# A two-layer decoder on one Trainium2 core: the second MLP product moved behind the whole first one, as one seven-product scheme summed in PSUM

## The chip, the core and the metric

The kernel runs on one core of one Trainium2 chip. The metric is the device time of one launch, in microseconds (us); less is better. Engines are named as in the profile: PE multiplies matrices (PEld are its weight loads), DVE, ACT and POOL work on elements, SP and POOL issue most transfers. SBUF is the memory on chip, PSUM the small one that PE sums into, in banks of 512 float32 columns by 128 partitions.

## What is computed

A decoder of two layers on 512 tokens of 1024 features, all in float32. Layer 0 mixes tokens by windowed means, layer 1 by a gated unit (SGU). Each layer's modulation comes from a vector c; each ends in an MLP with 4096 hidden features:

```python
def sq_relu_mlp(h, w1, w2):
    return jnp.square(jax.nn.relu(h @ w1)) @ w2

for i in range(DEPTH):
    mod = c_act @ ada_w[i] + ada_b[i]
    sh1, sc1, g1, sh2, sc2, g2 = jnp.split(mod, 6, axis=-1)
    h = modulate(rmsnorm(x, norm_mix_g[i]), sh1, sc1)
    y = pool_mixer(...) if kind == 0 else sgu_mixer(...)
    x = x + g1[:, None, :] * y
    h = modulate(rmsnorm(x, norm_mlp_g[i]), sh2, sc2)
    x = x + g2[:, None, :] * sq_relu_mlp(h, mlp_w1[i], mlp_w2[i])
return rmsnorm(x, final_g)
```

## The kernel before

*Precision.* Each float32 operand is held as a rounded high part and the rest (ACT copies the high part, `wh`, `hb`, `oh`; DVE subtracts it to get the low part, `wl`, `ol`), and `mm3` multiplies high by high, high by low and low by high. So one product is three matmuls, and each weight block of 128x1024 costs one ACT copy and one DVE subtraction (`split`); operands are treated alike by `parts`.

*The MLP*, function `mlp`, works in four chunks c of 1024 hidden features, of two quads j of 512 each. A unit is a piece of work whose matmuls stand together in PE's order:

- An **f unit** computes 128 hidden features of the first product plainly, 24 matmuls of 512 columns, for the first `FROM[i]` quads (3 in layer 0, 2 in layer 1).
- An **s unit** (c, j, m) is one of the seven products by which the other quads are multiplied (Strassen's scheme in Winograd's form; `ORDER` = 1, 5, 6, 3, 7, 2, 4), 24 matmuls of 256 columns. The running weight block is made by adding blocks: for m = 5 and 6 on DVE, for m = 4, and the block of m = 7, by accumulating transfers that POOL issues.
- A **p unit** (c, m) is one of seven products of the second product for chunk c = 0, 1, 2 (`ORDER2`), 24 matmuls of 512 columns: 4 pairs of blocks by two halves of the tokens by three parts. Its weights come from w2 as blocks of 1 MB: plain loads, and accumulating ones on POOL's queue that turn the same tile (`bt`) into the next sum (`CHAIN`). Each unit ends by adding both PSUM banks to y in SBUF (the first visit on ACT, the others on DVE).
- A **q unit** (dh, t) is a plain piece of the second product for chunk 3, 24 matmuls of 512 columns; eight of them, with the weights w2e.

Before, the p units of chunk c stand among the s and f units of chunk c+1, mostly one p unit and then one to three of those, and the q units end the layer. `gated` and `last1` add the result times the modulation's gate to x; `last1` also applies the final norm, and cuts the very last q unit into two parts of 256 columns.

*Other work under the MLP.* The columns of the adaLN product for the following stages (`ada`: a 512 KB load and one DVE instruction of 1024 columns each) are put in at the unit that `COLUMNS` gives.

*What sets the order.* PE's order is the program's. In layer 0, every operation of the MLP is recorded by `Plan` (so it bears line L130 in the profile; the others bear L102), and a list scheduler writes down a fixed order for all engines from a cost table: PE's order is given, each other engine takes the ready operation with the earliest due time. In layer 1 only PE's order is fixed, and the framework schedules the rest. Weight buffers `wh`, `wl` rotate over five.

Of the kernel before, what the change touches and what calls it, by code (L numbers as in the profile page):

```python
# [14 lines left out]
P = 128  # L15
D = 1024
# [13 lines left out]
SHIFT = {"o": 64, "q": 0, "g": 0}  # L30

# [40 lines left out]
COLUMNS = (0, 5, 8, 11, 13, 16, 19, 22, 25, 28, 30, 33, 36, 39, 42, 45, 47, 50, 53, 61, 61, 61, 61, 61)  # L72
LEAD = dict(SP=0.0, POOL=0.0, ACT=9.0, DVE=9.0, PE=13.0, fresh=7.0)
A_PARTS = (0, 0, 1, 2, 7)


class Plan:
# [125 lines left out]
    def run(self, lead):  # L203
# [63 lines left out]

        events, now, free, queue = [], 0.0, {e: lead[e] for e in ready}, 0.0
# [8 lines left out]
        while count < N:  # L277
            moved = True
            while moved:
                moved = False  # L280
                for e in ready:
# [4 lines left out]
                    else:  # L286
                        pick, back = None, []
                        while ready[e]:
                            k, i = heapq.heappop(ready[e])
                            if when[i] <= now + 1e-9 and fits(i):  # L290
                                pick = i
                                break
                            back.append((k, i))
# [24 lines left out]
                    heapq.heappush(events, (end, i))  # L318
                    moved = True
# [29 lines left out]
def decoder_kernel(ctx: ExitStack, tc: tile.TileContext, xtok, vecs, fgrow, ada0, ada1, pool_w, w1s, w1, w1f, w1b, w2, w2e, w_v, w_u, w_o, wsT, lnp, bs, out):  # L349
# [58 lines left out]
    def hparts(gap):  # L408
        t = big.tile([P, 2 * KD * S + GAP], F32R, name="hb", tag="hb")
        return t[:, GAP - gap : GAP - gap + 2 * KD * S].rearrange("p (h k s) -> p h k s", h=2, k=KD)  # L410

    h_ = [hparts(GAP)]

    shift(big, LINE - GAP)
# [9 lines left out]
    def H(k, c):  # L424

        return h_[0][:, 0, k, c], h_[0][:, 1, k, c]
# [558 lines left out]
    def mlp(i, first, extra, last, ending):  # L985
# [3 lines left out]
        with (  # L989
            tc.tile_pool(name="gq", bufs=3) as gq_,  # L990
            tc.tile_pool(name="su", bufs=1) as su_,
            tc.tile_pool(name="pad0", bufs=1) as pad0_,
            tc.tile_pool(name="op", bufs=2) as op_,
            tc.tile_pool(name="pad1", bufs=1) as pad1_,
            tc.tile_pool(name="w2p", bufs=3) as w2p_,
            tc.tile_pool(name="hx", bufs=1) as hx_,
            tc.manual_schedule(engines={PE} if i else ORDERED),
        ):
            gq, su, pad0, op, pad1, w2p, hx = (plan.pool(p, True) for p in (gq_, su_, pad0_, op_, pad1_, w2p_, hx_))
            plan.on = i == 0  # L1000
            shift(pad0, SHIFT["o"])
            shift(pad1, SHIFT["q"] - SHIFT["o"])
# [10 lines left out]
            def new_g(c, j):  # L1013
                g[c, j] = gq.tile([P, 4, S], F32, name="g", tag="g")

            def put(f, po):

                c, q = divmod(f, 8)
                j, p = divmod(q, 4)
                if p == 0:  # L1020
                    new_g(c, j)
                t = g[c, j][:, p]
                A.activation(in_row(t) if len(po.shape) == 2 else t.rearrange("p (r h s) -> p r h s", r=2, h=2), in_turn(po), AF.Relu)
                square(t)

            def quad(c, r, j):

                return g[c, j].rearrange("p a (h r t) -> p a h r t", h=2, r=2)[:, :, :, r]
# [19 lines left out]

            def a_parts(step):


                def a(r, j):
                    return xf[:, 4 * j : 4 * j + 4, 256 * r : 256 * r + 256]
# [16 lines left out]
                if m == 5:  # L1070
                    shift(hx, LINE - GAP)
                o = H(slice(0, 4), slice(256, 512)) if m == 7 else operand(*{5: (hx, "hx"), 6: (big, "x0"), 3: (big, "x1")}[m])
                parts(o, sums_a["t"].pop(m))
                sums_a[m] = o

            def a_sums(step):


                def a(r, j):
                    return h32[0][:, 4 * j : 4 * j + 4, 256 * r : 256 * r + 256]  # L1080

                def operand(pool, tag):
                    t = pool.tile([P, 2, 4, 256], F32R, name="as", tag=tag)
                    return t[:, 0], t[:, 1]

                def minus(o, p, q):
                    V.tensor_tensor(o, p, q, ALU.subtract)

                first, half = slice(0, 256), slice(256, 512)
                if step == 0:  # L1090
                    sums_a.update({1: H(slice(0, 4), first), 2: H(slice(4, 8), first), 4: H(slice(4, 8), half)})
                    shift(hx, LINE - GAP)
                    minus(a(1, 1), a(1, 0), a(1, 1))
                    m, o = 5, operand(hx, "hx")
                elif step == 1:
                    minus(a(1, 1), a(1, 1), a(0, 0))
                    m, o = 6, operand(big, "x0")
                elif step == 2:
                    minus(a(0, 0), a(0, 0), a(1, 0))
                    V.tensor_tensor(a(1, 1), a(1, 1), a(0, 1), ALU.add)  # L1100
                    m, o = 3, operand(big, "x1")
                else:
                    m, o = 7, H(slice(0, 4), half)
                parts(o, a(0, 0) if m == 7 else a(1, 1))
                sums_a[m] = o
# [7 lines left out]
            def blk(c, j, r, n):  # L1113
                if (c, j, r, n) not in blks:
                    blks[c, j, r, n] = raw4(w1b[quad_at(c, j), r, n])
                return blks[c, j, r, n]

            def s_prep(u):
# [20 lines left out]
                more = {1: [(c, j, 0, 1)], 5: [(c, j, 1, 1)], 3: [(c, j, 1, 0)], 7: [(*nxt, 0, 0)], 2: [(*nxt, 0, 1)], 4: [(*nxt, 1, 1)]}.get(m, [])  # L1139
# [7 lines left out]
            def s_run(u, w):  # L1147
# [13 lines left out]
                def block(r, n):  # L1161
                    return g[c, j][:, 2 * n : 2 * n + 2, 256 * r : 256 * r + 256]
# [17 lines left out]
            held = {}  # L1180

            def b_of(c, r, n, chain=False):
                kw = dict(name="bt", tag="bt", bufs=1) if chain else dict(name="b", tag="b", bufs=2)
                t = w2p.tile([P, 4, S], F32, **kw)
                Y.dma_start(t, w2[i, c, r, n])
                return t

            def b_add(t, c, r, n):
                G.dma_start(t, w2[i, c, r, n], accum_op=ALU.add)

            def p_prep(u):
                c, m = u
                B = held

                def s_tile(name):
                    return su.tile([P, 4, 2, P], F32, name=name, tag=name)

                if m == 1:
                    wb = B["t"] = b_of(c, 0, 0, True)
                    a = quad(c, 0, 0)  # L1200
                elif m == 5:
                    wb = B["t"]
                    a = B["s"] = s_tile("s")
                    V.tensor_tensor(a, quad(c, 1, 0), quad(c, 1, 1), ALU.subtract)
                elif m == 6:
                    wb = B["t"]
                    a = B["s"]
                    V.tensor_tensor(a, a, quad(c, 0, 0), ALU.subtract)
                    B["b12"] = b_of(c, 0, 1)
                    b_add(B["b12"], c, 1, 1)  # L1210
                    B["u"] = s_tile("u")
                    V.tensor_tensor(B["u"], quad(c, 0, 0), quad(c, 1, 0), ALU.subtract)
                elif m == 3:
                    wb = b_of(c, 1, 1)
                    a = B.pop("s")
                    V.tensor_tensor(a, quad(c, 0, 1), a, ALU.add)
                elif m == 7:
                    wb = B.pop("b12")
# [504 lines left out]
```

## Time and profile before

| | |
|---|---|
| Median of 3 runs | 817.22 us (816.99 to 818.46) |
| Span of the profiled execution | 814.3 us |
| Busy in the span | PE 798.3, PEld 723.5, DVE 686.5, ACT 486.7, POOL 69.1 us |
| Granted PE clock | 0.998 |
| Transfers | 185.47 MB, 228 GB/s |

The profiled execution has no time of its own beside its span; the runs' median lies 2.9 us above it, which covers what comes before the first and after the last recorded instruction. A span is counted from the first recorded instruction; "busy" is the sum of an engine's instructions, and instructions of DVE that follow each other overlap a little in the records, so that the price of one is the distance of two starts where the engine never waits. The page's chain goes back from the last instruction, at each step to what released it.

### The profile page before, as it was taken

The numbers are of one execution on the slowest core, as the hardware profiler recorded it, in microseconds if no ns is written. First come the engines' busy times: TensorE is split into PE (matmuls) and PEld (weight loads), VectorE is DVE, ScalarE is ACT, GpSimd is POOL, SyncE is SP. The second block draws the span as 40 slices with busy tenths as digits, with TensorE's granted clock in tenths as the row PEclk, the third lists the DMA queues.
The fourth block names the chain that finished last, engine by engine and source line by source line (L and its number), as shares of the span: only waits on it lengthen the run. The fifth ranks groups of instructions, "written<-read, shape, count | busy, mean of one in ns | idle before, by whom it ended". The sixth has DMA issues, their size and how long they took to land.

```text
span 814.3 us, 12668 instructions
## 1 busy us (share of the span) xinstructions
PE 798.3 (98%) x4909; PEld 723.5 (89%) x4909; DVE 686.5 (84%) x931; ACT 486.7 (60%) x708; POOL 69.1 (8%) x96
## 2 busy tenths in 40 slices
PE   6999999999999999999999999999999999999996
PEld 5678889999999999888889889999999999999985
DVE  5989888989999999866898886788789988987865
ACT  5476786766666676366233237776867666677521
POOL 4000011010100110000010001010101100111001
PEclk9999999999999999999999999999999999999999
DMA  9989988899898796537755646857888889887402
GB/s 352 417 297 327 403 226 174 274 223 278 233 271 247 185 279 225 195 111 252 242 184 208 219 155 241 302 109 207 206 260 218 230 226 252 212 176 249 139 1 104
DMA packets 43788, 185.47 MB, mean 228 GB/s; under 512 B 4920, under 2 KB 5072, under 8 KB 36432
## 3 DMA queue, kind: packets, MB, share of 16 engines
q1 hardware_dynamic: 35280, 137.72, 46.6%
q0 software_dynamic: 8016, 44.58, 27.4%
q10 hardware_dynamic: 432, 2.36, 0.7%
q8 instruction: 39, 0.64, 0.3%
q14 instruction: 21, 0.17, 0.1%
HBM read 178.33 MB, written 6.30 MB: 227 GB/s over the span
## 4 chain that ended last, share of the span: by engine, by line
PE 94%; DMA 2%; ACT 2%; DVE 1%; SPq 0%; issue 0%; POOLq 0%; ACTq 0%; DVEq 0%
PE po L102 39%; PE pm L102 19%; PE pm L130 18%; PE po L130 15%; PE px L102 1%; DMA x<-in_xtok 1%; PE pq L102 1%; DMA raw<-in_w1f 1%; ACT hb L102 1%; ACT h L102 0%; PE pt L102 0%; SPq L102 0%; DVE wl L102 0%; DVE hb L102 0%; PE ss L102 0%
## 5 line engine op out<-in xcount | busy, mean ns | idle before, releaser
L102 PE MATMUL po<-hb,wh 128*128 128x256 f32 (+1 forms) x816 | 175.9, 314 | 0.2 <-DVE hb L102 0.2
L102 PEld LDWEIGHTS po<-hb,wh 128*128 128x128 f32 x816 | 133.9, 191 | 9.0 <-DVE hb L102 1.1
L102 PE MATMUL po<-hb,wl 128*128 128x256 f32 (+1 forms) x408 | 126.2, 315 | 0.5 <-ACT hb L102 0.5
L102 DVE TENSOR_TENSOR wl<-raw,wh 128x1024 fp32r<-128x1024 f32 (+2 forms) x85 | 98.9, 1171 | 26.1 <-ACT wh L102 25.9
L102 ACT ACTIVATE wh<-raw 128x1024 fp32r<-128x1024 f32 (+2 forms) x85 | 85.4, 1016 | 45.7 <-PE pm L102 20.1
L130 ACT ACTIVATE wh<-raw 128x1024 fp32r<-128x1024 f32 x48 | 51.0, 1063 | 54.5 <-PE pm L130 22.0
L102 PEld LDWEIGHTS po<-hb,wl 128*128 128x128 f32 x408 | 76.7, 191 | 4.9 <-ACT hb L102 0.7
L130 PE MATMUL po<-hb,wh 128*128 128x256 f32 (+1 forms) x400 | 78.1, 296 | 0.0
L130 DVE TENSOR_TENSOR wl<-raw,wh 128x1024 fp32r<-128x1024 f32 x48 | 58.6, 1222 | 11.7 <-ACT wh L130 11.3
L102 DVE SCALAR_TENSOR_TENSOR ada<-ada,cb 128x1024 f32<-128x1024 f32 x50 | 60.6, 1219 | 6.5 <-DMA ada<-in_ada 6.3
L130 PEld LDWEIGHTS po<-hb,wh 128*128 128x128 f32 x400 | 63.7, 191 | 2.0
L130 PE MATMUL pm<-wh,oh 128*128 128x512 f32 x188 | 63.8, 357 | 0.0
L102 PE MATMUL pm<-wh,oh 128*128 128x512 f32 x188 | 63.8, 357 | 0.0
L102 PE MATMUL pm<-wh,ol 128*128 128x512 f32 x168 | 63.7, 379 | 0.0
L130 PE MATMUL pm<-wh,ol 128*128 128x512 f32 x168 | 63.7, 379 | 0.0
L130 PE MATMUL pm<-wl,oh 128*128 128x512 f32 x168 | 63.7, 379 | 0.0
L102 PE MATMUL pm<-wl,oh 128*128 128x512 f32 x168 | 63.7, 379 | 0.0
L130 PE MATMUL po<-hb,wl 128*128 128x256 f32 (+1 forms) x201 | 59.3, 296 | 0.0
L102 PE MATMUL po<-as,wh 128*128 128x256 f32 x288 | 49.0, 275 | 0.0
L102 PEld LDWEIGHTS po<-as,wh 128*128 128x128 f32 x288 | 43.8, 192 | 0.0
L130 PE MATMUL po<-as,wh 128*128 128x256 f32 x240 | 40.8, 275 | 0.0
L102 ACT ACTIVATE g<-g 128x512 f32<-128x512 f32 x50 | 31.5, 630 | 14.9 <-DVE g L102 14.2
(268 smaller groups left out, 1874.6 us busy)
## 6 DMA issues: line engine op xcount, KB each, us to landing
ada<-in_ada SPq DMA_DIRECT2D x76, 512.0 KB, 4.6
raw<-in_w1b SPq DMA_DIRECT2D x44, 512.0 KB, 5.8
b<-in_w SPq DMA_DIRECT2D x18, 1024.0 KB, 7.2
bt<-in_w POOLq DMA_DIRECT2D x18, 1024.0 KB, 8.5
raw<-in_w1b POOLq DMA_DIRECT2D x22, 512.0 KB, 6.5
raw<-in_w2e SPq DMA_DIRECT2D x16, 512.0 KB, 3.9
bt<-in_w SPq DMA_DIRECT2D x6, 1024.0 KB, 8.4
b<-in_w POOLq DMA_DIRECT2D x6, 1024.0 KB, 10.2
```

The costliest lines, as they stand in the source:

```text
L102: return f(*a, **kw)
L130: self.ops.append((name, attr, lambda: f(*a, **kw), out, ins, kw))
```

## The change

- The first product of a layer is finished first: f and s units of all four chunks. Then come 28 p units, seven products for each of four chunks, in this order: m = 1 and 2 for every chunk, m = 5 for all four, m = 6 for all four, a mixture of m = 3 and 7, and m = 4 at the end. q units and w2e are gone; w2 now holds all four chunks.
- The sums of the seven products stay in PSUM over the chunks (`start` at c = 0, `stop` at c = 3), and `evict` takes them out once, at chunk 3. The units (2,4) and (3,4) stand together, first for one half of the tokens, then for the other; `ending`, which starts the next layer's norm, is called between the halves. `last1` loses its narrow last part.
- All of g (the hidden features, 8 quads) stays in SBUF; operands and weight blocks move into tiles of x, hb and y that are free by then. Per layer, 1 MB blocks of w2 come as 12 plain and 16 accumulated transfers; before 12 and 12, and 4 MB of w2e.
- Layer 1's MLP is recorded and list-scheduled too (`PLAN`, `LEAD1`), with all queues in a fixed order; a rule `yields` lets DVE and ACT leave an operation for one that comes ready soon and is due sooner. `COLUMNS` puts the adaLN columns earlier.

Counted in the built programs: PE's matmuls 4749 before, 4636 after (those of the second product 1392 of 512 columns, where two of 256 count as one, and 1344); DVE's instructions of 1024, 512 and 256 columns 421, 253, 30 and 455, 168, 22; ACT's of 1024 and 512 columns 274, 302 and 300, 282.

```diff
-COLUMNS = (0, 5, 8, 11, 13, 16, 19, 22, 25, 28, 30, 33, 36, 39, 42, 45, 47, 50, 53, 61, 61, 61, 61, 61)
+COLUMNS = (0, 1, 2, 3, 5, 7, 8, 10, 12, 14, 16, 18, 20, 22, 24, 26, 28, 30, 32, 34, 36, 60, 61, 62)
+LEAD1 = dict(SP=0.0, POOL=0.0, ACT=9.0, DVE=9.0, PE=10.0, fresh=7.0)
+PLAN = (True, True)
...
+        def yields(e, i):
+            end = now + cost[i][0]
+            for j in soon[e]:
+                slack = late[j] - cost[j][1]
+                if j != i and eta[j] < end and slack < end and late[i] - cost[i][1] > max(slack, eta[j]) + cost[j][0]:
+                    return True
+            return False
...
-                            if when[i] <= now + 1e-9 and fits(i):
+                            if when[i] <= now + 1e-9 and fits(i) and not (e in ("DVE", "ACT") and yields(e, i)):
...
-            tc.manual_schedule(engines={PE} if i else ORDERED),
+            tc.manual_schedule(engines=ORDERED | ({mybir.EngineType.DVE, mybir.EngineType.Activation, mybir.EngineType.SP} if i and PLAN[1] else set())),
...
-            plan.on = i == 0
+            plan.on = PLAN[i]
...
             def p_run(u, ready):
-                halves = (0, 1)
                 c, m = u
                 o, w = ready
                 banks = XB if m in IN_X else ZB
-                start, stop = m in (1, 5, 2), m in (4, 3, 2)
+                start, stop = c == 0 and m in (1, 5, 2), c == 3 and m in (4, 3, 2)
...
-                for hf in halves:
-                    r, dh = TAKES[m]
-                    t = 2 * hf + r
-                    yt = y(t, dh)
-                    if (t, dh) in seen:
-                        V.tensor_tensor(yt, yt, banks[hf], ALU.subtract if minus else ALU.add)
-                    else:
-                        seen.add((t, dh))
-                        A.activation(yt, banks[hf], AF.Copy, scale=-1.0 if minus else 1.0)
...
+                if (c, m) == (2, 4):
+                    kept[u] = ready
+                    return
+                steps = [(p, hf) for p in range(4) for hf in range(2)]
+                if (c, m) in ((3, 7), (0, 4)):
+                    steps.sort(key=lambda x: x[1])
+                elif (c, m) == (3, 4):
+                    steps = [(p, hf) for hf in range(2) for p in range(-4, 4)]
+                for p, hf in steps:
+                    o, w = ready if p >= 0 else kept[2, 4]
+                    mm3(banks[hf], cut(o, ALL, p % 4, hf), pairs(w[p % 4 // 2], p % 2), start and p == 0, stop and p == 3, skip_group_check=True)
+                    if c == 3 and p == 3:
+                        evict(m, hf, banks[hf])
+                        if (m, hf) == (4, 0):
+                            ending()
...
-            for c in range(3):
...
-                for m, n in zip(ORDER2, step):
-                    units.append(("p", (c, m)))
-                    units += fs[0:n]
-                    fs = fs[n:]
-            units += [("q", (dh, t)) for dh in range(2) for t in range(NT)]
...
+            units += [("p", (c, m)) for c in range(4) for m in (1, 2)]
+            units += [("p", (c, m)) for m in (5, 6) for c in range(4)]
+            units += [("p", u) for u in ((0, 3), (1, 3), (0, 7), (2, 3), (1, 7), (3, 3), (2, 7), (3, 7))]
+            units += [("p", (c, 4)) for c in range(4)]
```

What this does to the orders is shown at three places. First DVE in layer 0's MLP, where s units run. Names: `wl` is the low part of a weight block, made from what stands behind the arrow (`raw`, `yr`, `tr`, `bt`, `b` are weight blocks as loaded), `ada` an adaLN column, `g` hidden features, `po` and `pm` PSUM banks of the first and second product, `ol` the low part of a p unit's operand. Before:

```order
L130 TENSOR_TENSOR wl<-raw,wh 128x1024
L130 TENSOR_TENSOR y<-y,pm 128x512 x2
L130 TENSOR_TENSOR wl<-raw,wh 128x1024
L130 TENSOR_TENSOR ol<-g,oh 128x1024
L130 TENSOR_TENSOR g<-g,po 128x2x256
L130 TENSOR_TENSOR wl<-bt,wh 128x1024
L130 SCALAR_TENSOR_TENSOR ada,pmv<-ada,cb 128x1024
L130 TENSOR_TENSOR mods_89<-pmv,vec 128x2
L130 TENSOR_TENSOR wl<-bt,wh 128x1024
L130 TENSOR_TENSOR y<-y,pm 128x512 x2
L130 TENSOR_TENSOR wl<-raw,wh 128x1024
```

After:

```order
L130 TENSOR_TENSOR wl<-tr,wh 128x1024 x2
L130 TENSOR_TENSOR g<-po,g 128x512
L130 TENSOR_TENSOR tr<-tr,yr 128x1024
L130 TENSOR_TENSOR g<-g,po 128x512
L130 SCALAR_TENSOR_TENSOR ada,pmv<-ada,cb 128x1024
L130 TENSOR_TENSOR wl<-tr,wh 128x1024
L130 TENSOR_TENSOR g<-g,po 128x512
L130 TENSOR_TENSOR tr<-tr,yr 128x1024
L130 SCALAR_TENSOR_TENSOR ada,pmv<-ada,cb 128x1024
L130 TENSOR_TENSOR mods_90<-pmv,vec 128x2
L130 SCALAR_TENSOR_TENSOR ada,pmv<-ada,cb 128x1024
```

The additions to y and the operands and weights of p units are gone from this place; weight splits of s units, additions of blocks (`tr<-tr,yr`) and adaLN columns now follow one another.

Second, POOL's queue in the MLP of layer 0, mostly accumulating transfers (`in_w1b` first product, `in_w` second). Before:

```order
L130 DMA bt<-in_w 128x2048 x2
L130 DMA raw<-in_w1b 128x1024
L130 DMA bt<-in_w 128x2048
L130 DMA raw<-in_w1b 128x1024
L130 DMA b<-in_w 128x2048
L130 DMA raw<-in_w1b 128x1024
```

After:

```order
L130 DMA yr<-in_w1b 128x1024
L130 DMA tr<-in_w1b 128x1024
L130 DMA bt<-in_w 128x2048
L130 DMA gain_1129<-line 8x128
L130 DMA bt<-in_w 128x2048 x6
L130 DMA gb<-gain_1129 128x1024
L130 DMA bt<-in_w 128x2048 x5
L130 DMA b<-in_w 128x1024 x4
```

The accumulations of the two products, which took turns, now stand apart: `yr` is the block of m = 7 and `tr` that of m = 4, one of each for every quad; behind them come `bt`, the running blocks of the p units, and `b`, their blocks of m = 7 (`gain` and `gb` belong to the modulation and do not accumulate).

Third, DVE at the end of the program, from one of the last evictions on (`tmp<-pm,gb` is the eviction times the gate, `cb` holds the final gain, `sums` and `rr` the norm). Before:

```order
L102 SCALAR_TENSOR_TENSOR tmp,sums<-x_7595 128x256
L102 TENSOR_SCALAR sums<-sums 128x1
L102 TENSOR_TENSOR x_7595<-x_7595,cb 128x256
L102 TENSOR_TENSOR tmp<-pm,gb 128x256
L102 TENSOR_TENSOR x_7595<-x_7595,tmp 128x256
L102 SCALAR_TENSOR_TENSOR tmp,sums<-x_7595 128x256
L102 TENSOR_TENSOR sums<-sums 128x1
L102 TENSOR_TENSOR x_7595<-x_7595,cb 128x256
L102 TENSOR_SCALAR x_7595<-x_7595,rr 128x512
```

After:

```order
L130 TENSOR_SCALAR sums<-sums 128x1
L130 TENSOR_TENSOR x_5039<-x_5039,cb 128x512
L130 TENSOR_TENSOR tmp<-pm,gb 128x512
L130 TENSOR_TENSOR x_5039<-x_5039,tmp 128x512
L130 SCALAR_TENSOR_TENSOR tmp,sums<-x_5039 128x512
L130 TENSOR_SCALAR sums<-sums 128x1
L130 TENSOR_TENSOR x_5039<-x_5039,cb 128x512
L130 TENSOR_SCALAR x_5039<-x_5039,rr 128x512
```

The last eviction and the two instructions behind it are 512 columns wide instead of 256; their number is the same.

358 lines of the change are left out of this document (159 added, 199 removed).

## The prediction

> **What bounds the kernel now.** I read the page's sums first, then the chain of waits that ended last, then stretches of the two MLPs.
>
> ```profile
> span 814.3 us, 12668 instructions
> ...
> PE 798.3 (98%) x4909; PEld 723.5 (89%) x4909; DVE 686.5 (84%) x931; ACT 486.7 (60%) x708; POOL 69.1 (8%) x96
> ...
> PE 94%; DMA 2%; ACT 2%; DVE 1%; SPq 0%; issue 0%; POOLq 0%; ACTq 0%; DVEq 0%
> ```
>
> PE is busy for 98% of the span and carries 94% of the chain. Is it also free of gaps inside the stretches that the change rewrites? The table of stretches (us from the span's start; sum, then busy time of PE, its weight loads, DVE, ACT and POOL; granted clock; DMA share; GB/s) says yes:
>
> ```profile
> 60.00:80.00 20.00, 20.00 (x94) 17.27 (x93) 20.00 (x31) 12.88 (x28) 0.00 (x0) 1.00 0.96 330
> 80.00:100.00 20.00, 20.00 (x95) 17.56 (x94) 16.25 (x20) 14.34 (x23) 0.00 (x0) 1.00 1.00 390
> 117.26:301.57 184.31, 184.31 (x1244) 172.56 (x1244) 169.50 (x194) 122.15 (x148) 17.77 (x21) 1.00 0.87 238
> 314.90:363.32 48.42, 48.42 (x234) 42.49 (x233) 38.34 (x67) 22.23 (x38) 2.12 (x4) 1.00 0.48 162
> 549.21:760.26 211.05, 211.05 (x1462) 198.71 (x1462) 182.72 (x195) 144.10 (x183) 19.20 (x24) 1.00 0.82 219
> 760.26:807.08 46.82, 46.81 (x242) 41.49 (x240) 33.07 (x51) 15.88 (x29) 1.70 (x3) 1.00 0.21 70
> ```
>
> In every row PE's busy time equals the stretch, at a granted clock of 1.00. So a matmul left out is worth its whole time as long as nobody is late, and everything else costs only where it makes PE wait. The covers are uneven: in the mixed stretch of layer 0 (third row) DVE is 92% busy and DMA 87%; in the plain chunks (fourth and sixth) DMA falls to 48% and 21%.
>
> **The change, part by part.** *Matmuls.* The chain, in order of time, gives the price:
>
> ```profile
> 304.36 5.19 PE pm L130 x25
> 309.55 5.36 PE po L130 x48
> 314.90 41.44 PE pm L130 x192
> ...
> 807.11 0.44 DVE tmp L102
> 807.57 0.44 DVE x L102
> 808.03 0.44 DVE tmp L102 x2
> 808.50 0.17 DVE sums L102
> 808.77 0.63 POOLq L1718
> 809.43 0.72 ACT x L102
> ```
>
> The third row is the plain chunk of layer 0: eight units, 192 matmuls of 512 columns, 41.44 / 192 = 0.2158 us each. A unit of the seven-product scheme has 24 of them and takes 5.19 us. The second product of a layer now has 3 x 7 x 24 + 192 = 696 matmuls, and then 4 x 7 x 24 = 672. Two layers: 48 fewer, 48 x 0.2158 = **-10.36 us**. The s units of the first product, two of them with 48 matmuls in 5.36 us by the second row, stay as they are. All of this lies on the chain.
>
> *Evictions.* Each seven-product unit of three chunks was added from PSUM into y. With sums held in PSUM over four chunks only the last chunk evicts. DVE's order has 85 fewer instructions of 512 columns and 34 more of 1024; ACT's 20 fewer and 26 more. DVE's prices when it never waits are read as distances between starts:
>
> ```profile
> 268.62 1.22 DVE L130 TENSOR_TENSOR wl<-raw,wh 128x1024 fp32r<-128x1024 f32 x1
> 269.75 0.68 DVE L130 TENSOR_TENSOR g<-po,g 128x512 f32<-128x512 f32 x1
> 270.35 0.68 DVE L130 TENSOR_TENSOR g<-g,po 128x512 f32<-128x512 f32 x1
> ...
> 282.53 1.22 DVE L130 SCALAR_TENSOR_TENSOR ada<-ada,cb 128x1024 f32<-128x1024 f32 x1
> 283.67 0.08 DVE L130 DVE_READ_ACCUMULATOR ada<-ada,cb 128x1 f32 x1
> 283.67 1.22 DVE L130 TENSOR_TENSOR raw<-raw 128x1024 f32<-128x1024 f32 x1
> ```
>
> That is 1.13 us per 1024 columns and 0.60 per 512: 34 x 1.13 - 85 x 0.60 = -13 us of DVE work over the program. ACT is 60% busy and has room for 26 more. On PE's chain: 0.
>
> *Where DVE's work now lies.* Counted in the order, the stage of s units of layer 0 (34 units from the first to the last, 34 x 2.68 = 91 us of PE) holds 71 DVE instructions of 1024 columns (35 weight splits, 21 adaLN columns, 10 additions of weight blocks, 5 others) and 14 of 512: 71 x 1.13 + 14 x 0.60 = 89 us, and about 0.1 us for each column's small additions makes 91. So DVE is full there. The stage of p units that follows has 101 and 29, 132 us of 145. Full is not late: in the first row of the stretches DVE was busy for 20.00 of 20.00 us and PE too. Who waits for whom there is told by the table of waits (total, times, longest):
>
> ```profile
> DVE wl L130 <- ACT wh L130: 16.4, 23, 1.4
> ACT wh L130 <- PE pm L130: 27.6, 23, 4.9
> ```
>
> DVE waits for ACT, and ACT for PE to give back a weight buffer: the splits run ahead of PE by all five buffers, of which an s unit uses one (some 10 us of cover). The 21 columns are needed only by the next layer. Bounds: 0, since nothing can be earlier than a PE without gaps; and, at the instructions' whole duration of 1.22 and 0.68 instead of their distance, 71 x 1.22 + 14 x 0.68 = 96 and the small ones, 98 - 91 = 7 us. I take 0.4, near the lower end, by the row with both engines at 20.00.
>
> *Transfers.* Per layer the 4 MB of plain loads for the plain chunk become 4 MB of accumulating ones.
>
> ```profile
> q1 hardware_dynamic: 35280, 137.72, 46.6%
> q0 software_dynamic: 8016, 44.58, 27.4%
> ...
> bt<-in_w POOLq DMA_DIRECT2D x18, 1024.0 KB, 8.5
> raw<-in_w1b POOLq DMA_DIRECT2D x22, 512.0 KB, 6.5
> ...
> b<-in_w POOLq DMA_DIRECT2D x6, 1024.0 KB, 10.2
> ```
>
> The first two rows (packets, MB, share of the 16 engines' span) give 0.466 x 814.3 / 137.72 = 2.76 us of the DMA engines for a plain MB and 0.274 x 814.3 / 44.58 = 5.0 for an accumulated one; the others end in the time from issue to landing. So +4 x (5.0 - 2.76) = +9 us of DMA per layer, in a stage of 145 us. It is thickest where the units of m = 5 and m = 6 run for four chunks each: eight accumulations of 1 MB, 40 us of DMA under 8 x 5.19 = 41.5 us of PE. The last four are wanted only by the units of m = 4 at the end, so I take 0; if they pushed the first four and a pair of plain loads (5.5 us) behind PE, it would be 40 + 5.5 - 41.5 = 4 us per layer, the upper bound; the lower is 0. The second row of the stretches, DMA share 1.00 under a PE of 20.00, speaks for 0.
>
> *The accumulated block of the s units' seventh product.* In every quad the unit of m = 5 adds block (0,1) on DVE, and POOL's queue then accumulates block (1,1) into it for m = 7. Three s units lie between, 3 x 2.68 = 8.0 us; before, a p unit or two lay there as well, 5 us each. Landing takes 6.5 us by the row of this very transfer. Queued behind it on POOL is only the accumulation for m = 4, which has four units' time. I take 0; below it nothing is to be had, and above, if it lands as late as the 10.2 us of the last row, 2.2 us in each of 5 + 6 quads, 24 us.
>
> *The seams.* A copy of 1024 columns on ACT is priced by its group (busy us, mean ns, idle time before it):
>
> ```profile
> L130 ACT ACTIVATE wh<-raw 128x1024 fp32r<-128x1024 f32 x48 | 51.0, 1063 | 54.5 <-PE pm L130 22.0
> ```
>
> At the change from s to p units the second p unit's operand goes into a buffer that the last s unit reads, so its ACT copy and DVE subtraction (1.06 + 1.13 = 2.2 us, by that mean and the distance on DVE above) come after that unit; the first p unit runs meanwhile for 5.19. Cost 0, bounds 0 and one more full instruction in the way on each engine, still 0. The list order in layer 1, formerly left to the framework on all queues but PE's, fixes DVE, ACT and SP too. The nearest row is layer 0's third stretch, where a fixed order ran PE without a gap: 0, up to what the last two paragraphs say.
>
> *The tail.* The last eviction is now 512 columns wide instead of two of 256, and what follows PE's last matmul runs alone:
>
> ```profile
> 802.72 0.69 DVE L102 TENSOR_TENSOR tmp<-y,gb 128x512 f32<-128x512 f32 x1
> 803.44 0.69 DVE L102 TENSOR_TENSOR x<-x,tmp 128x512 f32<-128x512 f32 x1
> ```
>
> Dependent instructions follow each other by 0.72 us at 512 columns here, and by 0.46 at 256 in the last rows of the chain (807.11, 807.57, 808.03). Three of them: 3 x 0.26 = **+0.78 us**. The product with the final gain becomes 512 wide too, but lies beside the 0.63 us of POOL in the chain.
>
> *Sum*, against the profiled execution: 814.3 - 10.36 + 0.78 + 0.4 = 805.1 us of span. The median of the runs, 817.22, lies 2.9 above that span, and I leave this offset: **808.0 us**, 1.1% less. What tells from no change here is about 0.2%, 1.6 us.
>
> **The rivals.** *Covers run out, partly.* DVE in layer 0's s units at 98 instead of 91 us, or DMA in m = 5 and 6, costs 2 to 6.5 us: 809.6 to 814.1, centre 811.5. For it: both loads are near 100% of their stage with no slack to spare. Against it: the rows at 20.00 and 1.00, and ten us of weight buffers.
>
> *Gone altogether.* If only layer 0's five quads wait the full 2.2 us for m = 7, and DVE, being full, can't catch up, 5 x 2.2 = 11 us eat the gain: 818, no change.
>
> *Slower: the accumulated block lands after its product in both layers.* Undoing the mixture of s and p units takes from m = 7 the p unit that hid its landing. At a landing of L us the 11 quads cost 11 x (L - 8.0); it decides from 8.0 + 9.2 / 11 = 8.8 us on, and at 10.2 gives 807.6 + 24 = 832. For it: 1 MB accumulations landed in 8.5 and 10.2, in a DMA that is now busier (5 MB accumulated in those 91 us). Against it: blocks of this size landed in 6.5 at a share of 0.87, and a late block first uses up the buffers ahead. The Trainium skill speaks for this side: "Perfetto Trace Analysis", section "Optimization Strategy", holds that where the most contended engine differs from stage to stage, interleaving the stages may help; the change does the opposite. By that rule this rival would have more weight than I give it; the trace agrees that the stages differ in their covers, but a PE that waits for none of them in either kind of stretch leaves the rule nothing to win.
>
> *The numbers.* The forecast has 0.71, partial loss 0.16, no change 0.04, slower 0.09. Faster by over 0.2%: 0.71 + 0.16 = 0.87; within: 0.04; slower: 0.09. The likeliest case alone spans 806.2 (no wait at all, 807.6, less 1.4 us, about what runs of one kernel differ by here, 816.99 to 818.46) to 809.6 (2 us of waits). The whole range, 806.2 to 814.2, takes in the partial loss; it leaves out the 0.13 of the last two rivals and a little at the ends.
>
> **What would show it.** PE's matmuls of the second product: 672 per layer and PE busy 10 us less. Stretches of s units in layer 0: PE at 20.00 of 20.00 with DVE near 20; a PE at 19 or below there, ended by DVE or by a split that waits for the accumulated block, is the first or third rival. DMA share near 0.95 where m = 5 and 6 run, with PE full. Between PE's last matmul and the end 0.8 us more than before. The prediction is wrong if PE, after losing its 48 matmuls, shows gaps of over 3 us inside the two MLPs, or if the chain there names DMA or DVE with more than a per cent.

## The result: 828.66 us, 1.4% slower

The changed kernel takes 828.66 us (median of 4 runs, 828.23 to 830.48) against 817.47 before (four runs by then, 816.99 to 818.46): ratio 1.0143, interval 1.0128 to 1.0157. The forecast was 808.0 and faster. Page sums and chain of the changed kernel:

```profile
span 827.2 us, 12433 instructions
...
PE 794.7 (96%) x4796; PEld 714.9 (86%) x4796; DVE 668.4 (81%) x870; ACT 499.8 (60%) x714; POOL 87.0 (11%) x112
...
PE 47%; DVE 17%; DMA 16%; issue 12%; ACT 4%; POOL 2%; SPq 1%; POOLq 0%; DVEq 0%; ACTq 0%
```

PE's share of the chain fell from 94% to 47%. PE is idle for 827.2 - 794.7 = 32.5 us instead of 16.0, 16.5 more; and though 10.4 us of matmuls are gone, its busy time fell by only 3.6, so that 6.8 us of longer busy time have come in. Together 16.5 + 6.8 - 10.4 = 12.9 us, the difference of the spans. Where is the new idle time? The rows of PE that waited (start, duration; in brackets the idle time just before and what ended it):

```profile
96.09 0.80 PE L130 MATMUL po<-hb,wl 128*128 128x256 f32 x2 [4.85 <-DVE wl L130]
217.73 0.38 PE L130 MATMUL po<-hb,wl 128*128 128x256 f32 x1 [2.48 <-DVE wl L130]
317.57 0.66 PE L130 MATMUL pm<-wh,op 128*128 128x512 f32 x1 [1.91 <-DVE op L130]
791.59 0.48 PE L130 MATMUL pm<-wh,op 128*128 128x512 f32 x1 [1.57 <-DVE op L130]
798.62 0.45 PE L130 MATMUL pm<-wh,op 128*128 128x512 f32 x1 [1.59 <-DVE y L130]
```

To these 12.4 of the 16.5 us come 2.4 at the seam of the layers (350 to 380 us) and 0.7 more than before at the start of layer 1's MLP; 1.0 lies in smaller gaps. And the busy time that should not be there? The granted clock (third figure from the right) in stretches of 2 us at two long gaps and a shorter one:

```profile
94.00:96.00 2.00, 0.00 (x0) 0.00 (x0) 2.00 (x4) 0.00 (x0) 0.00 (x0) 0.97 0.14 47
96.00:98.00 2.00, 1.91 (x6) 1.64 (x7) 2.00 (x3) 0.00 (x0) 0.00 (x0) 0.50 1.05 305
316.00:318.00 2.00, 0.43 (x1) 0.37 (x2) 1.51 (x2) 0.34 (x2) 0.00 (x0) 0.94 1.07 274
318.00:320.00 2.00, 2.00 (x6) 1.62 (x5) 1.19 (x2) 2.00 (x3) 0.00 (x0) 0.50 1.00 274
790.00:792.00 2.00, 0.42 (x3) 0.39 (x3) 2.00 (x3) 0.79 (x1) 0.00 (x0) 1.00 0.02 4
792.00:794.00 2.00, 2.00 (x11) 1.76 (x10) 2.00 (x3) 0.16 (x1) 0.00 (x0) 1.00 0.00 0
```

After each of the first three gaps the clock is at 0.50 for 3.41 us (the clock's own records). Half of that is lost, 1.7 us each time, 5.1 in all. The gaps of 1.6 us are not followed by one. Some 1.7 us of longer busy time stay unplaced.

**What ended each gap.** DVE at the first gap:

```profile
86.82 1.22 DVE L130 SCALAR_TENSOR_TENSOR ada<-ada,cb 128x1024 f32<-128x1024 f32 x1
87.96 0.09 DVE L130 DVE_READ_ACCUMULATOR ada<-ada,cb 128x1 f32 x1
93.67 1.23 DVE L130 SCALAR_TENSOR_TENSOR ada<-ada,cb 128x1024 f32<-128x1024 f32 x1 [5.62 <-DMA ada<-in_ada]
94.82 0.08 DVE L130 DVE_READ_ACCUMULATOR ada<-ada,cb 128x1 f32 x1
94.82 2.36 DVE L130 TENSOR_TENSOR wl<-raw,wh 128x1024 fp32r<-128x1024 f32 x2
```

DVE, 81% busy, stands still for 5.62 us in front of an adaLN column whose load has not landed, and the two splits that PE wants stand behind it, their high parts ready since 91.0. (The column's load was issued at 83.7 and landed 9.9 us later.) The third gap is the same on ACT:

```profile
308.36 0.16 DVE L130 SCALAR_TENSOR_TENSOR scl<-mods,vec 128x1 f32<-128x1 f32 x1
...
314.06 1.06 ACT L130 ACTIVATE wh<-b 128x1024 fp32r<-128x1024 f32 x1 [7.18 <-DMA b<-in_w]
315.02 1.04 ACT L130 ACTIVATE op<-g 128x1024 fp32r<-128x1024 f32 x1
315.15 1.23 DVE L130 TENSOR_TENSOR wl<-b,wh 128x1024 fp32r<-128x1024 f32 x1 [6.63 <-ACT wh L130]
316.30 1.22 DVE L130 TENSOR_TENSOR op<-g,op 128x1024 fp32r<-128x1024 f32 x1
```

The copy `op`, an operand from SBUF, waits behind the copy of a block that is 7 us late, and DVE behind ACT. That block comes out of a DMA that is full where p units run: its share is 0.99 there (second and fourth row below) against 0.78 in layer 0's s units (first row), and the second product's sums for m = 7 (`b` on POOLq) land 14.8 us after their issue. That the one causes the other is tested by e_plain.

```profile
100.00:200.00 100.00, 100.00 (x795) 97.05 (x794) 86.55 (x108) 69.98 (x100) 7.94 (x9) 1.00 0.78 242
220.00:340.00 120.00, 118.09 (x540) 103.03 (x540) 96.46 (x94) 73.62 (x80) 19.47 (x24) 0.98 0.99 243
560.00:640.00 80.00, 80.00 (x718) 80.00 (x718) 62.64 (x68) 56.80 (x84) 6.87 (x8) 1.00 0.66 191
680.00:780.00 100.00, 100.00 (x465) 87.58 (x464) 84.61 (x76) 63.09 (x66) 17.45 (x21) 1.00 0.99 235
...
bt<-in_w POOLq DMA_DIRECT2D x24, 1024.0 KB, 10.9
yr<-in_w1b POOLq DMA_DIRECT2D x11, 512.0 KB, 5.3
b<-in_w POOLq DMA_DIRECT2D x8, 512.0 KB, 14.8
```

In the second gap both meet. In the last quad two columns stand on DVE ahead of the split that frees the block `tr`, so POOL issues its last sum only at 204.44, just when SP's first loads for the p units go out:

```profile
198.03 1.22 DVE L130 SCALAR_TENSOR_TENSOR ada<-ada,cb 128x1024 f32<-128x1024 f32 x1
...
201.71 1.22 DVE L130 SCALAR_TENSOR_TENSOR ada<-ada,cb 128x1024 f32<-128x1024 f32 x1
...
202.92 1.23 DVE L130 TENSOR_TENSOR wl<-tr,wh 128x1024 fp32r<-128x1024 f32 x1
...
204.44 0.87 POOL L130 DMA_DIRECT2D tr<-in_w1b  x1 [5.17 <-DVE mods L130]
...
204.26 0.80 SPq L130 DMA_DIRECT2D bt<-in_w  x2
...
215.36 1.06 ACT L130 ACTIVATE wh<-tr 128x1024 fp32r<-128x1024 f32 x1 [4.01 <-DMA tr<-in_w1b]
```

The sum lands 10.9 us after its issue, where its kind takes 5.7 (median). Here the columns themselves were on time; it is their place ahead of the split that costs. In all eight profiles of this case (most of them of the experiments below) in which this sum lands over 10 us after its issue, PE's gap is that time less 8.4: 10.9 and 2.48 here, 12.3 and 3.86 in e_swap, 10.1 and 1.72 in e_dve6.

### The profile page after: what moved, and what is told of

Read it like the earlier page. It is cut to its first block, busy times and chain, and to the rows that moved or that the text cites. A ratio compares the mean times of both kernels' runs of the same rounds, so it can differ in the third digit from the quotient of the medians.

```text
span 827.2 us, 12433 instructions
## 1 busy us (share of the span) xinstructions
PE 794.7 (96%) x4796; PEld 714.9 (86%) x4796; DVE 668.4 (81%) x870; ACT 499.8 (60%) x714; POOL 87.0 (11%) x112
## 4 chain that ended last, share of the span: by engine, by line
PE 47%; DVE 17%; DMA 16%; issue 12%; ACT 4%; POOL 2%; SPq 1%; POOLq 0%; DVEq 0%; ACTq 0%
PE po L130 20%; PE po L102 17%; PE pm L130 7%; DVE wl L130 6%; DMA b<-in_w 4%; DMA g<-in_w 3%; DMA ada<-in_ada 3%; DMA bt<-in_w 2%; DMA tr<-in_w1b 2%; DVE op L130 2%; DVE g L130 2%; ACT wh L130 1%; DVE ada L102 1%; DMA yb<-in_w 1%; PE px L102 1%
## 5 line engine op out<-in xcount | busy, mean ns | idle before, releaser
L130 PE MATMUL pm<-wh,op 128*128 128x512 f32 x896 | 269.6, 381 | 5.6 <-DVE op L130 3.5
L130 PEld LDWEIGHTS pm<-wh,op 128*128 128x128 f32 x896 | 170.2, 190 | 31.9 <-DVE op L130 4.3
L130 PE MATMUL po<-hb,wh 128*128 128x256 f32 (+1 forms) x976 | 184.4, 293 | 0.6 <-DVE hb L130 0.6
L130 PE MATMUL pm<-wl,op 128*128 128x512 f32 x448 | 170.6, 381 | 0.0
L130 PEld LDWEIGHTS pm<-wl,op 128*128 128x128 f32 x448 | 85.0, 190 | 11.9
L130 DVE TENSOR_TENSOR op<-g,op 128x1024 fp32r<-128x1024 f32 x56 | 68.4, 1224 | 17.6 <-ACT op L130 17.6
L130 DVE TENSOR_TENSOR wl<-bt,wh 128x1024 fp32r<-128x1024 f32 x64 | 77.0, 1223 | 4.0 <-ACT wh L130 4.0
L130 ACT ACTIVATE wh<-bt 128x1024 fp32r<-128x1024 f32 x64 | 66.9, 1052 | 16.9 <-PE pm L130 14.3
L130 PE MATMUL po<-as,wl 128*128 128x256 f32 x264 | 72.7, 275 | 0.1
L102 PE MATMUL po<-hb,wh 128*128 128x512 f32 x240 | 71.6, 380 | 0.0
## 6 DMA issues: line engine op xcount, KB each, us to landing
bt<-in_w POOLq DMA_DIRECT2D x24, 1024.0 KB, 10.9
bt<-in_w SPq DMA_DIRECT2D x16, 512.0 KB, 10.2
```

The source lines that it names most:

```text
L102: return f(*a, **kw)
L130: self.ops.append((name, attr, lambda: f(*a, **kw), out, ins, kw))
```

## The experiments

All are edits of the changed kernel; ratios are to the kernel before, run on the same chip. The changed kernel itself ran on one chip; the kernel before took 816.8 to 817.5 us on all five, so differences against 828.66 are good to about 0.7 us beside the scatter of the runs. A profile shows one execution, and places of gaps are read from it.

| run | edit | us | ratio (interval) |
|---|---|---|---|
| e_swap | two splits ahead of the second column | 824.50 | 1.0094 (1.0072 to 1.0116) |
| e_pool | sums in recorded order | 836.03 | 1.0232 (1.0194 to 1.0271) |
| e_add | last quad's sum on DVE | 826.13 | 1.0119 (1.0097 to 1.0141) |
| e_free1 | layer 1 not list-scheduled | 850.89 | 1.0414 (1.0388 to 1.0439) |
| e_plain | p units' sums as plain loads (other result) | 822.03 | 1.0060 (1.0042 to 1.0077) |
| e_floor | e_swap, e_add, e_plain (other result) | 813.95 | 0.9952 (0.9934 to 0.9970) |
| e_dve6 | four 0.5 MB additions per layer on DVE | 823.26 | 1.0073 (1.0057 to 1.0089) |
| e_best | e_swap, e_add, e_dve6 | 819.46 | 1.0030 (1.0011 to 1.0049) |
| e_price | dearer transfers in the planner | 824.26 | 1.0082 (1.0068 to 1.0097) |
| e_move | seven columns later | 816.15 | 0.9987 (0.9973 to 1.0001) |
| e_addk | e_add, e_dve6, e_price | 817.43 | 1.0009 (0.9991 to 1.0027) |
| e_addck | e_addk, columns into the p units | 826.01 | 1.0117 (1.0104 to 1.0130) |
| f_dve6 | e_move, e_dve6 | 812.41 | 0.9953 (0.9941 to 0.9965) |
| f_dve6p | f_dve6, e_price | 817.09 | 1.0001 (0.9992 to 1.0009) |
| f_all | f_dve6, e_add | 812.85 | 0.9959 (0.9943 to 0.9974) |

**e_swap.** In the planner's list, the starts of the two `wl` behind the second `ada` of layer 0's MLP are set just ahead of it; all queues but DVE's stay.

> The changed kernel with one edit in DVE's order: at the start of layer 0's MLP two weight splits stand ahead of the second adaLN column instead of behind it; all other queues are as they were. Theory (a fixed order lets the column's late load hold up splits that are ready): the 4.85 us gap of PE at 91.2 us goes, and with it the 3.41 us of halved clock behind it, 1.7 us; 828.7 - 6.5 = 822. Rival (the transfers are too slow there, and the next weight load is late whoever stands first): the gap moves by a few units, 827 to 829.

824.50: the gap is gone, and with it the low clock. The stretch 88 to 98 us in the changed kernel and in this run, then this run's second gap:

```profile
88.00:98.00 10.00, 5.15 (x22) 4.12 (x21) 4.38 (x7) 4.06 (x6) 0.00 (x0) 0.89 0.84 318
...
88.00:98.00 10.00, 10.00 (x49) 8.79 (x48) 7.20 (x8) 6.14 (x9) 0.00 (x0) 1.00 0.97 389
...
214.09 0.38 PE L130 MATMUL po<-hb,wl 128*128 128x256 f32 x1 [3.86 <-DVE wl L130]
```

The theory is right on the cause: the column's load landed at 93.2 us, in the changed kernel at 93.6, so hardly sooner, and PE did not wait. But the time falls by only 4.2 of the 6.5 us. In the profile the second gap grew from 2.48 to 3.86, and a halved clock stands at the seam; the third place, on the other hand, has no wait, although ACT, POOL and SP have layer 0's old order.

**e_pool.**

```diff
...
+                            if i in sums_left and i != sums_left[0]:
+                                back.append((k, i))
+                                continue
...
```

> The changed kernel with the planner's accumulating transfers kept in the order in which they are recorded: the 1 MB sums for m = 4 are issued behind the 512 KB sums for m = 7 that are needed before them. Theory (in the p units DMA moves urgent sums behind ones that have 40 us of time): the gap at 315.7 us (1.9 us and 1.7 us of halved clock) goes and the one at 790.0 (1.6) too; 828.7 - 5.2 = 823.5. Rival (the sum of the transfers is the bound): the sums for m = 4 come late in turn, and the gaps move into the last four units; 828 to 831.

836.03, worse than the rival's 828 to 831. In one thing the theory is right: the sums for m = 7 land 5.4 to 11.6 us after issue instead of 12.2 to 19.2, and the waits at 315 and 790 are gone. The new waits are not the rival's either: they lie in unit (3,3) of both layers, ahead of the last four units, and end with splits of a block for m = 3.

```profile
338.93 0.69 DVE L130 TENSOR_TENSOR x<-x,tmp 128x512 f32<-128x512 f32 x1 [4.73 <-DMA x<-xd]
339.54 4.62 DVE L130 TENSOR_TENSOR wl<-g,wh 128x1024 fp32r<-128x1024 f32 x4
...
340.81 0.79 PE L130 MATMUL pm<-wl,op 128*128 128x512 f32 x1 [6.16 <-DVE wl L130]
...
790.51 0.69 DVE L130 TENSOR_TENSOR x<-x,tmp 128x512 f32<-128x512 f32 x1 [2.56 <-DMA x<-xd]
...
792.39 0.80 PE L130 MATMUL pm<-wl,op 128*128 128x512 f32 x1 [3.99 <-DVE wl L130]
```

`x<-xd` is the 1 MB reload of x, which POOL issues among the sums. It lands 17.4 us after its issue instead of 8.4 (layer 1: 15.2 instead of 8.6), DVE's instruction on it is first in its queue, and the splits stand behind it, three high parts ready since 335.8. It is the first gap once more, with another load. The sums for m = 4 themselves, issued last, made PE wait nowhere.

**e_add.**

```diff
-                if m in (5, 6):
+                if m in (5, 6) or m == 4 and (c, j) == (3, 1):
                     V.tensor_tensor(t, t, b(*CHAIN[m]), ALU.add)
...
-                if m == 6:
+                if m == 6 and (c, j) != (3, 1):
                     add(t, *CHAIN[4])
```

> The changed kernel with the last quad's block for m = 4 of the first product added by DVE (one more 1024-column instruction per layer) instead of by an accumulating transfer. Theory (that transfer shares the DMA engines with the first loads of the p units and lands in 10.9 us instead of 5.4): the gap at 215.3 us (2.5 us and 1.7 us of halved clock) goes; 828.7 - 4.2 = 824.5. Rival (the p units' own first blocks are late too): the gap moves to the first p units, 827 to 829.

826.13, 2.5 us less: between theory and rival. The 2.48 us gap has turned into 1.36, 0.73 and 0.62 in the first p units, none with a halved clock. In this run's first gap, which the edit does not touch, PE waited 2.61 instead of 4.85 us.

**e_free1.** `PLAN = (True, False)`.

> The changed kernel with layer 1's MLP left to the framework's order on DVE, ACT and SP, as before the change; layer 0 as changed. Theory (layer 1's gaps, 1.6 us at 790.0, 1.6 at 797.0 and 1.0 at its start, come from late transfers and evictions, not from a fixed order): 827 to 831. Rival (the list order in layer 1 is what costs): gaps there go, 824 to 825.

850.89, neither. Without the list order the kernel is 22 us slower, with gaps of 8.42 us at 788, 3.55 at 524 and 2.84 at 809, all in layer 1's part. The fixed order that hurts at late transfers is worth more than it costs there.

This run tells something else. Its layer 0 has the changed kernel's order on every queue, and yet its three places show 4.60, 1.93 and no wait, for 4.85, 2.48 and 1.91; at the third, the first sum for m = 7 landed 11.0 us after its issue instead of 14.1. So gaps differ between executions of the same order, and the third one comes and goes. That it is missing from the profile of an edited kernel does not show that the edit removed it.

**e_plain and e_floor.** In `record`, the call drops `accum_op` for all tiles but `yr` and `tr`. These two kernels leave out the sums of the second product's blocks and compute something else; they only price the transfers.

> The changed kernel with every accumulating transfer of the second product's blocks issued from the same place of the same queue as a plain load of the same block; so the running blocks are replaced instead of summed, and the second product is another one. Order and everything else as they were. Theory (16 accumulations a layer at over 5 us of DMA fill the p units' stage): DMA share there falls from about 1.0 to some 0.75, the gaps at 315.7 and 790.0 and the 1.7 us of halved clock go; 828.7 - 5.2 = 823.5; the gaps at 91 and 215 us stay. Rival (those gaps come from the order of the queue, not from how long a sum takes): they stay, 828 to 829.

> The changed kernel with three edits: two weight splits ahead of the second adaLN column on DVE, the last quad's block for m = 4 added by DVE, and the second product's accumulating transfers as plain loads (its blocks are replaced instead of summed). Theory (the 48 matmuls are worth 10.4 us as soon as no one is late): no gap over 1.7 us in the MLPs and no halved clock there; what stays are the seam (2.2 us), layer 1's start and last eviction (2.6); 817 - 10.4 + 0.8 + 4.8 - 0.8 for the gaps that the kernel before has too = 811.5. Rival (a p unit now costs PE more than 5.19 us, so something beside the waits is lost): 815 or more.

e_plain 822.03, 1.5 under the theory. DMA share and PE in the p units of both layers:

```profile
220.00:340.00 120.00, 120.00 (x557) 105.30 (x557) 100.42 (x95) 76.66 (x84) 12.41 (x24) 0.99 0.67 239
680.00:780.00 100.00, 100.00 (x465) 87.57 (x464) 84.90 (x76) 63.00 (x66) 10.58 (x20) 1.00 0.62 219
```

PE's gaps at 315 and 790 are gone; those at 92 and 214 stay, 2.92 and 2.90 us. The third place alone would prove little, but the blocks for m = 7 now land 3.9 to 6.8 us after issue in layer 0 instead of 14.1 to 19.2. So what an accumulation costs DMA, in the same queue and order, makes the block late. e_floor 813.95, 2.5 above the theory: what is left lies at the seam (2.2 us of gaps and a halved clock) and in gaps under 1 us.

**e_dve6.**

```diff
-                if m in (1, 5):
+                if m == 1 or m == 5 and c > 1:
                     sum_in(chain[c], c, *CHAIN[m + 4 if m == 1 else 6])
...
+                    for q in range(2 if c < 2 else 0):
+                        V.tensor_tensor(flat(chain[c], q), flat(chain[c], q), kept[c][q], ALU.add)
```

> The changed kernel with the running block for m = 6 of the first two chunks added on DVE from the block of m = 3, which is in SBUF by then (four more 1024-column instructions per layer) instead of by two accumulating transfers of 1 MB. Theory (DMA is the bound in the p units): 10.5 us of DMA less per layer, the gaps at 315.7 (1.9 and 1.7 of halved clock) and 790.0 (1.6) go: 823.5. Rival (DVE is as full as DMA there): as many us of waits for DVE instead, 828 to 831.

823.26: right to 0.3 us as a time, and DMA's share in the two p stages fell from 0.99 to 0.90 and 0.89. The gaps at 315 and 790 are gone too, but the first sum for m = 7 lands 11.2 us after its issue, about as in e_free1 without the edit, so that part of the theory is not shown.

**e_best.**

> All three edits that keep the computation: splits ahead of the second adaLN column, the last quad's block for m = 4 added by DVE, and the block for m = 6 of two chunks added by DVE. Theory (three independent waits, each with its halved clock): 828.7 - 6.5 - 4.2 - 5.2 = 812.8, faster than the kernel before by 0.5%. Rival (the waits are one shortage of DMA and DVE that moves on when a place is mended): 819 to 825.

819.46: the rival. In the profiled run, at 822.61 one of the longer of runs from 815.06 to 825.56, the first two places are quiet, but the third waits again, and a new wait comes up in the s units, each with a halved clock:

```profile
173.93 0.38 PE L130 MATMUL po<-hb,wl 128*128 128x256 f32 x1 [1.89 <-DVE g L130]
314.23 0.48 PE L130 MATMUL pm<-wh,op 128*128 128x512 f32 x1 [1.86 <-DVE op L130]
```

Mended alone, the three gave 4.2, 2.5 and 5.4 us, 12.1 together; at once they gave 9.2.

**e_price and e_move.**

```diff
-            return (5.05 * mb, 3.6 + 4.8 * mb) if kw.get("accum_op") else (2.7 * mb, 0.9 + 5.2 * mb)
+            return (5.4 * mb, 4.6 + 5.4 * mb) if kw.get("accum_op") else (2.9 * mb, 2.2 + 5.2 * mb)
```

```diff
-COLUMNS = (0, 1, 2, 3, 5, 7, 8, 10, 12, 14, ...
+COLUMNS = (0, 5, 6, 7, 8, 9, 10, 11, 12, 14, ...
```

> The changed kernel with dearer transfers in the planner's cost table alone (an accumulated MB 5.4 instead of 5.05 us of DMA and 10 instead of 8.4 to land, a plain one 2.9 instead of 2.7 and 7.4 instead of 6.1, the measured ones); the order that comes out has the first two weight splits ahead of the second adaLN column by itself. Theory (the fixed order is wrong where the table took a transfer for landed that was not): the gap at 91 us goes, 6.5 us, and the waits for late blocks stay: 822. Rival (late data is late in any order and new waits come up elsewhere): 826 to 829.

> The changed kernel with the adaLN columns 1 to 7 put in at units 5 to 11 instead of 1 to 10, the rest as it was. Theory (it was the second column so early that held up the splits): the gap at 91 us goes, as in the run that only swapped two rows, 822 to 825. Rival (DVE is full in the s units, and every column moved later into them costs a wait there): 826 to 829.

e_price 824.26: the gap at 91 is gone, others come (2.7 us at the seam, 2.1 and 1.0 at 754). Between the two. (The expectation calls its prices measured; for 1024 KB accumulated the pages give 5.25 us before and 5.09 in the changed kernel, not 5.4.)

e_move 816.15: 12.5 us by seven numbers, far more than the theory, and the kernel before is reached. The first three gaps have gone, not one. Of the second this can be read: with one column ahead of the split instead of two, the last sum is issued at 195.78, before SP's first loads for the p units at 198.98, and lands in 5.3 us instead of 10.9.

```profile
189.15 0.86 POOL L130 DMA_DIRECT2D yr<-in_w1b  x1 [11.50 <-DVE tr L130]
195.78 0.87 POOL L130 DMA_DIRECT2D tr<-in_w1b  x1 [5.77 <-DVE wl L130]
```

The third is the wait that also goes without any edit; here its sums land 10.7 to 16.5 us after issue, as in e_free1 (11.0 to 16.7).

**e_addk and e_addck.** In the second, `COLUMNS` has six columns more at units 40 to 53.

> The dearer transfers in the planner's table together with the two DVE additions (the last quad's block for m = 4, the block for m = 6 of two chunks). Theory (the planner knows of the late blocks, and DMA has 10.5 us less per layer): at least as good as the three edits by hand that gave 819.5, 814 to 819. Rival (DVE, with 5 more instructions per layer, is the bound in layer 0): 820 to 824.

> The same with six of the adaLN columns moved from layer 0's s units to its p units (DVE 7 us less in the first, as much more in the second). Theory (the gaps that come up in the s units once the first is gone, 1.9 us at 172 in the kernel with three edits, are DVE's, which is full there): those gaps go, 2 to 4 us less than the kernel without the move, 812 to 816. Rival (DMA is what is short, and in the p units more so): the same or up to 3 us more.

e_addk 817.43, within the theory. e_addck 826.01: the rival, and worse than it said, 8.6 us more than e_addk instead of up to 3. PE waits 4.28 and 2.33 us at the seam for the next layer's operands, which need the last columns; DVE itself waits 3.35 us for the load of one.

**f_dve6, f_dve6p, f_all.**

> The kernel with the adaLN columns 1 to 7 moved, and in it the block for m = 6 of two chunks added by DVE instead of by accumulating transfers (10.5 us of DMA less per layer). Theory (what the moved columns left in the p units, 0.8 us at 336 and 0.8 at 777, is DMA's lateness, and the scatter of its runs, 813 to 820, comes from there too): 814 to 815.5, runs closer together. Rival (only seam, evictions and layer 1's start are left, none of them DMA's): 816 or, with the added DVE work, 817.

> The same with the measured, dearer prices of transfers in the planner's table. Theory (an order made for late transfers waits less): 812 to 815. Rival (the order was already right there, and every new order makes its own gaps, as in the run with the prices alone): 815 to 822.

> The kernel with moved columns, the block for m = 6 of two chunks and the last quad's block for m = 4 added by DVE. Theory (with the columns moved, the last quad's sum landed in 5.3 us and needs no help): the same as without that last edit, within 1.5 us. Rival (that sum is still close to late): 2 us less.

f_dve6 takes 812.41 us (811.70 to 814.02) and is faster than both kernels: by 0.5% than the one before, on the same chip, and by 2.0% than the changed one (812.41 / 828.66). Its page:

```profile
span 810.0 us, 12425 instructions
...
PE 788.1 (97%) x4796; PEld 710.8 (88%) x4796; DVE 676.7 (84%) x878; ACT 500.7 (62%) x714; POOL 81.5 (10%) x108
...
PE 79%; DVE 9%; DMA 5%; ACT 4%; issue 2%; SPq 0%; POOLq 0%; POOL 0%; ACTq 0%; DVEq 0%
```

PE's busy time is 10.2 us under that of the kernel before: here the forecast saving of 10.36 shows, since no clock is halved in the MLPs. What is given back is idle time, 21.9 us against 16.0; the longest gap in the MLPs, 1.87 us at 305, is at the third place once more. The theory is right in direction and the gain larger than it said (814 to 815.5): the runs lie closer together (five, over 2.3 us, against ten over 7.0), and DMA's share in layer 1's p units is 0.89 (665 to 765 us, the part of the stage that 680 to 780 was above) instead of 0.99. The dearer prices (817.09) make new gaps, the rival; the last quad's sum (812.85) adds nothing, as expected.

## Why the prediction was wrong

The forecast had 1.2 us for waits and tail; 23.3 came, 16.5 of idle time and 6.8 of longer busy time. Both signs of being wrong that it named came too: a gap of 4.85 us in an MLP, and a chain with DVE at 17% and DMA at 16%.

- **Matmuls, -10.36 us: right.** f_dve6 has the saving in PE's busy time; e_floor and f_dve6 are faster than before.
- **"Full is not late", DVE's +0.4: the step that failed.** It asked how much DVE does in the s units' stage. But in the rows above a queue in a fixed order waited as a whole for the operand of its first instruction, with ready splits behind it. The right question was what stands in front of the splits, and when its load lands. At 91 us that was a column whose load ran at a DMA share of 0.96 (80 to 91 us) and landed after 9.9 us; I had quoted just that stretch of the kernel before, at 0.96 and 1.00, as proof that a full DMA is harmless. It was harmless with the order of before. Around 200 us it was two columns that delayed the issue of the last sum. Measured: 6.6 us at 91 (gap and clock), 4.2 at 215; e_swap shows the first, by order alone, and e_move, which moves the columns, gives 12.5 back. The ten us of weight buffers did not help at 91: the first two high parts of the stage were made at 88.5 and 90.0, so nothing was stored ahead.
- **Transfers in the p units, taken as 0 with an upper bound of 4 per layer: wrong end.** The mechanism was that of the bound, sums wanted later ahead of sums wanted sooner (e_pool turns that round, and the first sum for m = 7 lands 5.5 us after issue instead of 14.1), but the wait came one stretch later than I had put it, among m = 3 and 7. It cost 3.6 us in layer 0's profile, where it comes and goes, and 1.6 in layer 1's; e_plain and e_dve6 take 6.6 and 5.4 off the time. I also priced a block at 5.0 us, but it has 1024 KB, 1.05 of the page's MB: 5.25 us, more than the 5.19 of a p unit. It was a partial-loss rival to which I gave 0.16.
- **The s units' block for m = 7, 0: right.** It lands in 5.3 us (median), under the 8.0 that it has; the slowest of eleven took 9.0, and PE did not wait for it. So the slower rival had the right sign by a wrong mechanism; it was the block for m = 4, with four units of time, that came late, once.
- **Evictions, 0 on PE's chain: not quite.** At 797 us PE waited 1.59 us for an eviction (`y`) that stands in DVE's queue behind two subtractions for operands, and 0.53 at the same unit of layer 0.
- **Seam and list order, 0:** 2.4 us of gaps at the seam and 0.7 at the start of layer 1's MLP. The list order in layer 1 is on the whole a gain, of 22 us (e_free1).
- **Tail, +0.78:** from PE's last matmul to the end 7.6 us, 7.2 before: +0.4. The offset of 2.9 us was not all head and tail of a run: a run's time lies 1.7 us above its own span (828.89 and 827.2 here), and the other 1.2 say that the execution profiled before was faster than the median.
- **The halved clock** was in no term: 5.1 us, and 1.7 us of longer busy time stay open.
- **The rule that I weighed**, that of the Trainium skill, "Perfetto Trace Analysis", section "Optimization Strategy" (interleave stages with different bounds), deserved the weight that I denied it. Mixed, DMA was at 0.87 and 0.82 of its time; apart, it is at 0.99 in the p units and 0.78 and 0.66 in the s units. That PE waited for nothing before showed that the mixture worked, not that it was needless. Nor is it needed: f_dve6 keeps the stages apart and is faster than the kernel before.

## What to carry to other kernels

When an order is fixed ahead, price each instruction at the head of a queue by when its operand lands, not by how long the engine works; put work that nobody waits for behind the work that the bound engine needs, but not so late that the next stage waits for it (e_addck). A stage with no gaps says nothing of the gaps after its transfers are moved: divide DMA's work by stage, in the units of the blocks themselves. Count a gap of PE with the slow clock that follows it. And before you credit an edit with a gap that is gone from one profile, look whether another execution of the unedited order has it.

## What the hardware showed beside this

The clock's records lie on a grid of 3.41 us. I laid that grid over PE's busy time in the traces of both kernels and all fifteen experiments and took the windows at full clock: all 44 in which PE was busy for at most 0.40 of the time (start and end of the programs among them) were followed by a window at 0.50; of the 12 between 0.42 and 0.48 seven were, and of the rest none. So a gap of 1.86 us inside one window halves the clock (e_best, at 312), one of 1.87 us does not (f_dve6, at 305; busy 0.51 of its window), and neither does one of 2.92 us that falls on the edge of two windows (e_plain, at 92). The Trainium skill, "TensorE: Matmul & The Clock Gate", Part 1, tells of such a free-running window of about 3.4 us and of half clock after an idle one; the traces agree with both numbers, but the window need not be idle.
